# Hybrid decoder trunk on one core: eight-row norm factors and ACT-queue weights at the opening, another place for turning x and a halved last tile at the end

## Chip, cores and metric

One core of a Trainium2 chip runs the whole program in one launch. The metric is device time in microseconds (us), median over runs. One execution was also profiled; its span is the time from the first to the last instruction that the profile shows, and the execution's own time is a little longer than that. In what follows PE is TensorE (matrix products and transposes), PEld its weight loads, DVE VectorE, ACT ScalarE, POOL GpSimd, and SP SyncE, which here only issues DMAs. "SPq" and "POOLq" are DMAs issued by SP and POOL.

## The reference

Two layers over 512 tokens of width 1024. Each layer has a half-step SwiGLU block, a mixing block with three groups of heads, and another half-step SwiGLU block:

```python
for l in range(DEPTH):
    x = x + 0.5 * swiglu(rms_norm(x, ffn1_norm[l]), ffn1_w_in[l], ffn1_w_out[l])
    h = rms_norm(x, mix_norm[l]) @ w_mix_in[l]
    ...
    x = x + y @ w_mix_out[l]
    x = x + 0.5 * swiglu(rms_norm(x, ffn2_norm[l]), ffn2_w_in[l], ffn2_w_out[l])
return x
```

with `rms_norm(x, gain) = x * rsqrt(mean(x*x) + eps) * gain` and `swiglu(h) = (silu(gate) * up) @ w_out`, where gate and up are the two halves of `h @ w_in` (2 x 2816 columns). All is float32. The change concerns the very first block (layer 0, ffn1) and the very last one (layer 1, ffn2), and the loads of the norm gains in between.

## The kernel before

**Products.** Every operand is split into a high and a low part (`hi`, `lo`, in a rounded 32-bit form), and `mm3` makes three PE products of each: hi by hi (L346), hi by lo (L352), lo by hi (L353). `parted` makes the parts of streamed weights: ACT copies the rounded high part (L334), DVE subtracts it for the low part (L335).

**x.** Inside the kernel x lies transposed: `xT` has eight tiles of 128 features by 512 tokens. x comes from memory as tokens by features, so at the opening `load_x` loads the columns of one feature tile (one 256-KB DMA, L1543, into `xs`) and PE turns them with four 128x128 transposes into a PSUM bank (L1546). At the end `turn_x` turns `xT` back (L1509: 8 output tiles with four transposes each) and ACT copies each bank out (L1514).

**Streaming.** `stream` and `stream_steps` walk over the rows of a weight matrix in granules of two row tiles. `granule` loads one into a buffer `st` (two buffers, issued by SP, L315), parts it into `hl` (three buffers), and the products of four jobs (four PSUM banks) follow. Without the flag `end` the order is row tile by row tile, and within each the jobs; in the last granule it is job by job, so that the banks finish one after the other.

**The first block's opening.** `cover` streams the first six tiles of the hidden width in three rounds (f = 0, 2, 4). In the first (`opening`) the callback `pre` is `open_x`: at granule k it applies the gain to x's tiles k and k + 1 out of PSUM (`norm_part`: ACT's high part L420, DVE's low part L421) and, halfway through the granule, loads and turns the next two, copies x to `xT` (L1535) and adds up squares (L431, L434, L435). The gain of a norm is loaded by `begin_norm` (L409) into a tile of 128 partitions by 8, feature k*128 + p at partition p, column k: 1024 single elements from memory. `signs` (L632) makes a negated copy, `ngain`. While `open_x` works, `build_consts` fills masks on DVE and POOL. The `table` call that loads ACT's function table is the program's first statement.

The norm itself is not applied before the products. After the first round `squares` (L454) sums the squares over features into a bank with the tag `po`, ACT and DVE form the reciprocal root (L461 to L446, ending on DVE), and later steps multiply it in. The second round's fourth job writes a bank with the same tag, of which there is one.

**The order.** `follow` chains instructions of one engine into the order of the program text; where it isn't used, a scheduler orders them by priority. From the third round on most work follows a plan (`halved`, `plan`) with the loads `w` (L785, L703) chained on SP's queue. That part isn't touched.

**The last block's end.** In `ffn`, after `cover`, six row tiles of `w_out` remain, streamed in three granules for each half `dg` of the output columns. The last block computes tokens by features directly: first `turn_x` is issued as a whole, its banks all of one tag with two or three banks (`("mm", "sc")[self.ntog % 2]`, here `sc`, two banks), then 72 products for each half into four banks (`mm`, `mm`, `mm`, `po`, then `sc`, `sc`, `pt`, `pt`). DVE adds half of each bank to x (L504) and SP writes the 128x512 tile out (L508).

Of the kernel before, what the change touches and what calls it, by code (L numbers as in the profile page):

```python
# [23 lines left out]
P = 128  # L24
# [157 lines left out]
class Trunk:  # L182
# [32 lines left out]
    def build_consts(self, scratch):  # L215
# [40 lines left out]
        for l in range(1, 7):  # L256
            nc.vector.tensor_scalar(a, xf, scalar1=float(2 ** (l - 1)), scalar2=None, op0=ALU.is_ge)
# [22 lines left out]
    def table(self, name):  # L280
# [5 lines left out]
        self.tab = p.ins.name  # L286
# [15 lines left out]
    def granule(self, parts, kk, ahead=True, skew=0, keep=False):  # L302

# [8 lines left out]
        at = 0  # L312
        for ap in parts:
            w = ap.shape[1]
            nc.sync.dma_start(s3[:, :, at : at + w], ap.rearrange("(k p) c -> p k c", p=P))  # L315
            at += w
        with self.tc.high_priority() if ahead else ExitStack():
            hi, lo = self.parted(st[:, : kk * c], 1 if ahead else kk, skew, keep)
# [3 lines left out]
    def parted(self, src, pieces=1, skew=0, keep=False):  # L322
# [9 lines left out]
        for c in range(0, n, w):  # L332
# [28 lines left out]
    def stream_steps(self, jobs, parts_of, act, nk, mid=None, pre=None, deal=None, keep=False):  # L361
# [11 lines left out]
        while k < nk:  # L373
            kk = min(2, nk - k)
            if callable(mid) and k == nk - 2:
                mid()
            if pre is not None:
# [4 lines left out]
            rows = self.granule(parts_of(k, kk), kk, pre is None, skew, deal is not None)  # L382
            end = k + kk == nk
            order = (
                [(job, j) for job in jobs for j in range(kk)]
                if end
                else [(job, j) for j in range(kk) for job in jobs]
            )
            for n, ((acc, cols, toks, *more), j) in enumerate(order):
# [4 lines left out]
                first, last = k + j == 0 and not more, end and j == kk - 1  # L394
                if toks is None:
                    self.mm3(acc, hi[:, cols], lo[:, cols], ah, al, first, last, False, keep)
                else:
                    self.mm3(acc, ah[:, toks], al[:, toks], hi[:, cols], lo[:, cols], first, last)
# [7 lines left out]
    def begin_norm(self, gain_ap):  # L406
        nc = self.nc
        self.gain = self.const.tile([P, KD], F32, tag="gain", name=self.n("gain"), bufs=2)
        nc.sync.dma_start(self.gain, gain_ap.rearrange("(k p) -> p k", p=P))  # L409
        self.sqacc = None  # L410

# [54 lines left out]
    def ffn(self, w_in, w_out, next_gain, covered, mean=None, begin=None, out=None):  # L466
# [5 lines left out]
        with tc.tile_pool(name=self.n("ffn"), bufs=1) as fp:  # L472
# [11 lines left out]
            if last:  # L484
                xs = self.turn_x()
            for dg in range(2):
# [7 lines left out]
                self.stream(  # L494
# [5 lines left out]
                )  # L500
                if last:
                    for i in range(4):
                        o = self.xo[dg * 4 + i]
                        nc.vector.scalar_tensor_tensor(  # L504
                            out=o, in0=banks[i], scalar=0.5, in1=xs[dg * 4 + i],
                            op0=ALU.mult, op1=ALU.add,
                        )
# [1092 lines left out]
```

## Time and profile before

| | |
|---|---|
| median of 3 runs | 1847.46 us (1845.98 to 1848.6) |
| profiled execution, its own time | 1847.27 us |
| its span | 1845.3 us |
| PE busy in it | 1826.9 us, 99% |
| DVE, ACT, POOL busy | 80%, 55%, 10% |
| bytes moved by DMA | 254 MB, mean 138 GB/s |

The page of the profile lists busy times by engine, the span in 40 slices, DMA queues, the chain of work that ended last, and groups of instructions with mean durations. Other views of the same trace show instructions in order of time, waits with what ended them, and busy times in chosen stretches. PE's products overlap in its pipeline, so that the spacing of their starts, not their listed duration, is what one costs.

### The profile page before, as it was taken

The page shows a single profiled execution, that of the slowest core. Times are in us where ns is not written, and L with a number is a line of the kernel's source. Part 1 is how long each engine was busy: PE and PEld are TensorE (multiplying, and loading weights), DVE is VectorE, ACT ScalarE, POOL GpSimd, SP SyncE. Part 2 cuts the span into 40 slices and gives each one's busy share as a digit, 9 for nine tenths or more (in the row PEclk, how much of TensorE's full clock was granted, in tenths as well). Part 3 has the DMA queues.
Part 4 walks back from the last instruction along what each step waited for, and adds up shares of the span by engine and source line. Part 5 has one row for each costly group of instructions (what it writes and reads, how often), then busy time and mean ns, then how long its engine had stood idle before and what let it go on. Part 6 is the DMA issues. An engine that isn't in the chain of part 4 may idle for free.

```text
span 1845.3 us, 33378 instructions
## 1 busy us (share of the span) xinstructions
PE 1826.9 (99%) x13532; PEld 1698.6 (92%) x13532; DVE 1476.5 (80%) x2101; ACT 1005.9 (55%) x1462; POOL 182.5 (10%) x186
## 2 busy tenths in 40 slices
PE   8999999999999999999999999999999999999999
PEld 6899999899877899999889999998998788999997
DVE  7889787678787988879678887966868878888883
ACT  4455554564665555555445555545546665555552
POOL 0011120100000101112001111201000001020210
PEclk9999999999999999999999999999999999999999
DMA  7658783332323767868276787823323238677762
GB/s 205 183 126 194 178 177 92 69 96 72 76 75 98 215 136 175 186 169 172 81 201 139 169 188 184 172 61 89 81 64 87 81 103 228 151 158 195 150 137 91
DMA packets 247529, 254.00 MB, mean 138 GB/s; under 512 B 19632, under 2 KB 232112, under 8 KB 247376
## 3 DMA queue, kind: packets, MB, share of 16 engines
q1 hardware_dynamic: 191664, 183.69, 33.4%
q0 software_dynamic: 55712, 68.18, 23.2%
q8 instruction: 106, 1.74, 0.4%
q14 instruction: 47, 0.39, 0.1%
HBM read 226.08 MB, written 2.10 MB: 124 GB/s over the span
## 4 chain that ended last, share of the span: by engine, by line
PE 91%; DVE 4%; ACT 3%; issue 1%; DMA 1%; SPq 0%; ACTq 0%; DVEq 0%
PE mm L346 13%; PE mm L353 13%; PE mm L352 13%; PE sc L346 6%; PE sc L353 6%; PE sc L352 6%; PE pt L346 6%; PE pt L352 6%; PE pt L353 6%; PE po L346 3%; PE po L352 3%; PE po L353 3%; PE po L1449 1%; DVE hl L335 1%; ACT hl L334 1%
## 5 line engine op out<-in xcount | busy, mean ns | idle before, releaser
L732 ACT CAST hl<-w 128x1024 fp32r<-128x1024 f32 x322 | 337.7, 1050 | 346.9 <-PE mm L353 81.7
L734 DVE TENSOR_TENSOR hl<-w,hl 128x1024 fp32r<-128x1024 f32 x322 | 392.7, 1220 | 86.5 <-ACT hl L732 86.4
L335 DVE TENSOR_TENSOR hl<-st,hl 128x512 fp32r<-128x512 f32 (+2 forms) x196 | 166.5, 851 | 118.3 <-ACT hl L334 117.3
L334 ACT CAST hl<-st 128x512 fp32r<-128x512 f32 (+2 forms) x196 | 146.6, 750 | 206.9 <-PE mm L353 67.4
L346 PE MATMUL mm<-xc,hl 128*128 128x256 f32 (+1 forms) x730 | 201.3, 276 | 0.3 <-ACT g L831 0.3
L353 PE MATMUL mm<-xc,hl 128*128 128x256 f32 x728 | 201.2, 276 | 0.0
L352 PE MATMUL mm<-xc,hl 128*128 128x256 f32 x728 | 201.1, 276 | 0.0
L346 PE MATMUL sc<-xc,hl 128*128 128x256 f32 (+1 forms) x530 | 146.3, 277 | 0.6 <-ACT g L831 0.6
L353 PE MATMUL sc<-xc,hl 128*128 128x256 f32 x528 | 146.0, 277 | 0.0
L352 PE MATMUL sc<-xc,hl 128*128 128x256 f32 x528 | 145.9, 276 | 0.0
L346 PEld LDWEIGHTS mm<-xc,hl 128*128 128x128 f32 x730 | 137.1, 188 | 0.8 <-ACT g L831 0.5
L353 PEld LDWEIGHTS mm<-xc,hl 128*128 128x128 f32 x728 | 136.7, 188 | 0.1
L352 PEld LDWEIGHTS mm<-xc,hl 128*128 128x128 f32 x728 | 136.7, 188 | 0.0
L352 PE MATMUL pt<-xc,hl 128*128 128x256 f32 x480 | 132.6, 276 | 0.0
L346 PE MATMUL pt<-xc,hl 128*128 128x256 f32 (+1 forms) x482 | 132.6, 276 | 0.0
L353 PE MATMUL pt<-xc,hl 128*128 128x256 f32 x480 | 132.5, 276 | 0.0
L346 PE MATMUL mm<-hl,x 128*128 128x256 f32 (+1 forms) x384 | 112.4, 293 | 0.7 <-DVE ft L442 0.3
L346 PE MATMUL mm<-x,hl 128*128 128x512 f32 x272 | 109.7, 403 | 0.0
L353 PE MATMUL mm<-hl,x 128*128 128x256 f32 (+1 forms) x384 | 107.6, 280 | 0.0
L352 PE MATMUL mm<-hl,x 128*128 128x256 f32 (+1 forms) x384 | 107.3, 279 | 0.0
L353 PE MATMUL mm<-x,hl 128*128 128x512 f32 x272 | 106.5, 392 | 0.0
L352 PE MATMUL mm<-x,hl 128*128 128x512 f32 x272 | 106.0, 390 | 0.0
(470 smaller groups left out, 5677.1 us busy)
## 6 DMA issues: line engine op xcount, KB each, us to landing
w<-in_ffn_w_in_dram SPq DMA_DIRECT2D x140, 512.0 KB, 5.7
w<-in_ffn_w_out_dram SPq DMA_DIRECT2D x64, 512.0 KB, 4.4
w<-in_ffn_w_out_dram POOLq DMA_DIRECT2D x56, 512.0 KB, 8.9
st<-in_w_mix_in_dram SPq DMA_DIRECT2D x88, 256.0 KB, 2.7
w<-in_ffn_w_in_dram POOLq DMA_DIRECT2D x39, 512.0 KB, 8.4
st<-in_ffn_w_in_dram SPq DMA_DIRECT2D x72, 256.0 KB, 3.3
w<-S POOLq DMA_DIRECT2D x35, 512.0 KB, 4.7
st<-in_ffn_w_out_dram SPq DMA_DIRECT2D x24, 512.0 KB, 4.1
```

The costliest lines, as they stand in the source:

```text
L334: a = nc.scalar.copy(hi, src[:, c : c + w])
L335: b = nc.vector.tensor_sub(lo, src[:, c : c + w], hi)
L346: i = nc.tensor.matmul(acc[:, c], ah, bh[:, c], start=first and c.start == 0, stop=False, skip_group_check=True,)
L352: nc.tensor.matmul(acc, ah, bl, start=False, stop=False, skip_group_check=True)
L353: i = nc.tensor.matmul(acc, al, bh, start=False, stop=last, skip_group_check=True)
L732: A(nc.scalar.copy(hi, src))
L734: return lambda: V(nc.vector.tensor_sub(lo, src, hi))
L1449: nc.tensor.matmul(self.ob[:, t0 + u * P : t0 + 2 * P], V[:, j, h % 4].rearrange("p a d -> p (a d)"), part[:, j, u:, :].rearrange("p i t - ...
```

## The change

At the opening:

- The gain of the first norm is loaded as eight rows of 128 (`gr`, 8 DMA rows of 512 bytes in place of 1024 elements), first on SP's queue; PE transposes it and DVE copies it into `gain`.
- The first granule of weights is issued by ACT, in four DMAs of 128 KB (one for each row tile and part), ahead of ACT's table load, which moves from the program's first statement to this place. SP's queue is put into one order by `follow`.
- x's tile k + 1 is scaled between the two halves of the granule's parting (`between`), so that ACT and DVE take tile k, weights k, tile k + 1, weights k + 1.
- DVE's work on one of the masks is put behind the first granule's parting (`first_rows`).
- In the second round the first granule is done job by job (`lead`).

At the end:

- `turn_x` becomes a generator that turns four tiles at a time, over two banks each of `sc` and `pt`, one step after each of the first two granules.
- In the last granule of the second half the last job's products are done in two halves of 256 columns, and its tile is added and written in two halves (`last`).

Between them, the later gains' loads are chained on SP's queue (`follow` in `begin_norm`); they come after the loads `w` of the block that precedes them, where they came earlier before, and the negated copies on DVE move with them.

```diff
-    def granule(self, parts, kk, ahead=True, skew=0, keep=False):
+    def load_rows(self, parts, kk, queue=None):
...
+        for k in [slice(i, i + 1) for i in range(kk)] if queue is nc.scalar else [slice(0, kk)]:
+            at = 0
+            for ap in parts:
+                w = ap.shape[1]
+                d = (queue or nc.sync).dma_start(
+                    s3[:, k, at : at + w], ap.rearrange("(k p) c -> p k c", p=P)[:, k, :]
+                )
+                at += w
+                if queue is not None:
+                    self.follow("a" if queue is nc.scalar else "s", d)
+        return st[:, : kk * c]
...
+            if pieces > 1 and c == 0:
+                self.between()
...
             if pre is not None:
+
+                if k == 0:
+                    st = self.load_rows(parts_of(k, kk), kk, self.nc.scalar)
+                    self.table(LNEXP)
+                    self.follow("a", self.tab_ins)
                 pre(k)
...
-                if end
+                if end or lead and k == 0
...
+            if halves:
+                acc, cols, toks = jobs[-1]
+                for c in (slice(0, T // 2), slice(T // 2, T)):
+                    for j in range(kk):
+                        ah, al = act(k + j)
+                        hi, lo = rows[j]
+                        self.mm3(
+                            acc[:, c], ah[:, toks], al[:, toks], hi[:, c], lo[:, c], False, j == kk - 1
+                        )
...
-        nc.sync.dma_start(self.gain, gain_ap.rearrange("(k p) -> p k", p=P))
         self.sqacc = None
+        if pool is None:
+
+            self.follow("s", nc.sync.dma_start(self.gain, gain_ap.rearrange("(k p) -> p k", p=P)))
+            return
+        g = pool.tile([KD, P], F32, tag="S", name=self.n("gr"), bufs=2)
+        self.follow("s", nc.sync.dma_start(g, gain_ap.rearrange("(k p) -> k p", p=P)))
+        b = self.bank("pt")
+        self.follow("p", nc.tensor.transpose(b[:, :KD], g, self.ident[:KD, :KD]))
+        self.follow("v", nc.vector.tensor_copy(self.gain, b[:, :KD]))
...
-                xs = self.turn_x()
+                xs = []
+                turn = self.turn_x(xs, (("mm", "mm"), ("sc", "pt"))[self.ntog % 2])
...
+                    last=last and dg == 1,
+                ):
+                    if last:
+                        next(turn, None)
...
+                        cs = [slice(0, T)]
+                        if dg and i == 3:
+                            cs = [slice(0, T // 2), slice(T // 2, T)]
...
+                self.begin_norm(gain, fp)
                 self.xb = {j: self.load_x(x, j, fp) for j in (0, 1)}
-                self.begin_norm(gain)
-            for j in (k, k + 1):
-                self.norm_part(j, fp, self.xb[j], 0)
+            self.norm_part(k, fp, self.xb[k], 0)
+
+            self.between = lambda: self.norm_part(k + 1, fp, self.xb[k + 1], 0)
             return
```

More of the change, by code (lines that the diff above doesn't have):

```diff
@@ L359, in stream, with stream_steps @@
             pass
[L361 removed]
+    def stream_steps(self, jobs, parts_of, act, nk, mid=None, pre=None, deal=None, keep=False, lead=False, last=False):
         k = 0
@@ L599, in cover @@
                 None if opening else (lambda k, f=f: deal(2 * f + k // 2)), begin is None or f > 2,
+                lead=f == 2 and begin is not None,
             )
```

63 lines of the change are left out of this document (36 added, 27 removed).

## Prediction

> **What bounds the kernel now.** I read the page first, then stretches of busy time at both ends, the chain of waits there, and the instructions in order of time.
>
> ```profile
> span 1845.3 us, 33378 instructions
> PE 1826.9 (99%) x13532; PEld 1698.6 (92%) x13532; DVE 1476.5 (80%) x2101; ACT 1005.9 (55%) x1462; POOL 182.5 (10%) x186
> ```
>
> TensorE (PE) sets the time. No product is removed, so only places where PE waits or runs slowly can pay: 18.4 us in all (1845.3 - 1826.9), part of it in the middle, where the change puts nothing but small gain loads. The run profiled took 1847.27 us, 1.97 more than its span, and lies 0.19 under the median of the runs, 1847.46. I work from 1847.27.
>
> ```profile
> 8.45:13.60 5.15, 5.15 (x16) 4.22 (x17) 5.14 (x10) 2.19 (x4) 0.00 (x0) 1.00 1.10 316
> 13.60:35.60 22.00, 22.00 (x107) 18.34 (x106) 19.56 (x44) 11.90 (x19) 1.44 (x1) 1.00 0.85 233
> 35.60:41.00 5.40, 4.60 (x18) 3.13 (x18) 3.73 (x6) 4.18 (x5) 0.00 (x0) 1.00 0.47 151
> 1800.00:1803.75 3.75, 3.75 (x35) 3.75 (x35) 3.75 (x4) 1.66 (x2) 0.00 (x0) 1.00 0.35 125
> 1803.75:1810.20 6.45, 5.77 (x41) 4.55 (x40) 1.94 (x3) 4.95 (x8) 0.00 (x0) 1.00 0.53 171
> 1810.20:1841.55 31.35, 31.31 (x138) 25.56 (x137) 8.33 (x11) 3.75 (x4) 0.00 (x0) 1.00 0.19 67
> 1841.55:1845.30 3.75, 0.00 (x0) 0.00 (x0) 0.69 (x1) 0.00 (x0) 0.00 (x0) 1.00 0.37 140
> ```
>
> Columns: stretch, length, busy time and count of PE, PEld, DVE, ACT, POOL, clock, DMA share, GB/s. From 8.45 to 35.60 PE has no gap. The losses are: ahead of 8.45; a slow pace until about 13.6, which this view's clock column does not show; 0.8 us after 35.60; the stretch 1803.75 to 1810.20, whose 5.77 also counts PE's pipelined overlap; and the 3.75 us behind the last product.
>
> **The opening.** In order of time, then from the chain:
>
> ```profile
> 0.75 1.28 ACT L282 ACT_TABLE_LOAD   x1 [0.75 <-PEq L1585]
> 1.80 0.51 SPq L409 DMA_DIRECT2D gain<-in_ffn_norm_dram  x1
> 2.35 1.52 SPq L315 DMA_DIRECT2D st<-in_ffn_w_in_dram  x2
> 3.91 1.75 SPq L1543 DMA_DIRECT2D xs<-in_x_dram  x2
> 6.31 1.26 ACT L420 ACTIVATE x<-mm,gain 128x512 fp32r<-128x512 f32 x2 [4.27 <-DMA gain<-in_ffn_norm_dram]
> 7.74 1.14 ACT L334 CAST hl<-st 128x512 fp32r<-128x512 f32 x2 [0.16 <-DMA st<-in_ffn_w_in_dram]
> 8.45 1.11 PE L1546 MATMUL mm<-ident,xs 128*128 128x128 f32 x4 [2.67 <-DMA xs<-in_x_dram]
> 9.87 0.78 PE L346 MATMUL sc<-x,hl 128*128 128x512 f32 x1
> ...
> 9.56 0.66 PE po L1546 x3
> 10.22 0.43 PE sc L346
> 14.72 0.23 PE sc L346
> 20.20 0.87 PE mm L1546 x8
> ...
> 16.31 1.44 POOL L707 DMA_DIRECT2D w<-in_ffn_w_in_dram  x1 [14.66 <-DMA w<-in_ffn_w_in_dram]
> ```
>
> ACT waits for the gain until 6.31, PE for the third tile of x until 8.45, and the first product starts at 9.87. A product takes 0.43 us at first and 0.23 later (0.2275 as a mean: 31.35 us for 138 in the stretch from 1810.20); a transpose takes 0.22 slow and 0.109 fast (0.66 for three, 0.87 for eight). The twelve products of x's first tile and the eight transposes of x's third and fourth tiles are over at 14.72.
>
> Now the eight rows of factors go out first on SP, and the four loads of the first granule leave SP for ACT. So x's third tile is issued after one small load and two tiles, some 1.7 us earlier (four issues near 0.5 us put it near 2.2, against 3.91). Does it land so much earlier? The bytes bound that:
>
> ```profile
> 1.75:4.00 2.25, 0.31 (x2) 0.34 (x3) 1.11 (x8) 0.28 (x1) 0.00 (x0) 1.00 0.86 232
> 4.00:8.45 4.45, 1.78 (x9) 1.09 (x7) 2.17 (x14) 1.98 (x4) 0.00 (x0) 1.00 0.89 252
> 10.00:15.00 5.00, 5.00 (x17) 3.95 (x16) 3.69 (x6) 1.92 (x4) 0.00 (x0) 1.00 1.12 319
> ```
>
> Before 8.45 the engines moved 2.25 x 232 + 4.45 x 252 = 1643 KB. Three tiles of x and the first granule are 1311 KB (five times 256 KB, in thousands). At the mean of 245 GB/s that takes 5.35 us from 1.75, so 7.1; at 319 it is 5.9. To either comes the time from last packet to semaphore, some 0.5 us by my estimate (the output tile shown below is issued behind DVE's end at 1842.24, lands 2.0 later, and its packets end by 1843.8). That gives 6.4 to 7.6, and 8.0 if later tiles mix in. I take 7.3, nearer the slow end, because the 512-byte packets of x are in the slow rows. Two slow transposes bring the first product to **7.75**.
>
> The operands must be there. The factors: one load's landing is at most 4.4 us in the opening (the wait above ends at 6.2 after an issue at 1.80), so 5.2 at worst, then a transpose and a copy of 8 columns, 0.3 to 0.5 each counting handover; 6.2 at worst. ACT issues four loads at 0.5 to 0.76 each (SP's 1.52 for two) and loads its table (1.28): free by 5.1. Then a cast of x (0.63) and one of weights (0.57): 7.4 at worst, before the first product. No row shows a DMA issued by ACT.
>
> The pace: PE worked without a gap from 8.45, and sped up near 13.6, 5.15 us later. By the same bytes, shared equally between the queues, x's first tile is there near 4.5 (524 KB moved) and its second near 6.2 to 6.5 (1048 KB). If the gapless run now starts with the second at 6.2, the pace rises at 11.3. From 7.75, eight products at 0.43 end at 11.2, four at 0.2275 at 12.1, six transposes at 0.109 at 12.75. Against 14.72 that is **2.0 us**. Lower end: the pace rises at 13.6 as before and the start slips to 8.5: twelve products at 0.43 end at 13.7, six transposes at 14.3, 0.4. Upper end: start at 7.2, and the run counts from x's first tile at 4.5, so fast from 9.65: 3.0.
>
> The Trainium skill ("TensorE: Matmul & The Clock Gate", section "Part 1: The HAM clock gate (the "warmup" mystery)") says that the array runs at half rate until a free-running window of about 3.4 us has been busy, so the moment hangs on the window's phase and not on the first matmul alone. By that rule the rise is 3.4 to 6.8 us after steady work begins, an estimate of 9.6 to 13.0 here, and the opening would bring 1.2 to 3.0 instead of 2.0. The trace's 5.15 agrees with it.
>
> Behind that nothing should stall: the loads of the second x group and granule keep their places ahead of the 512-KB prefetches, and those prefetches move later on SP.
>
> **The first norm's wait.** Chain after the sum of squares (35.60 to 36.47, x2):
>
> ```profile
> 35.60 0.87 PE po L454 x2
> ...
> 39.51 0.70 DVE nt L442
> ...
> 40.25 0.50 PE po L346
> ```
>
> The fourth job's bank (po) holds the sum until DVE's L442 has read it at 40.21, 3.74 us after the sum's end. From 36.47 to 40.75 PE does 14 products, worth 3.19 of 4.28 us: 1.09 lost; by idle time 0.80 (the row 35.60:41.00). Afterwards the granule runs job by job: 18 products, 4.10 us, come ahead of po, more than 3.74. Gain **0.95**, ends 0.8 and 1.09; with the cover of 0.36 us gone it would shrink by what is missing.
>
> **Turning x at the end.**
>
> ```profile
> PEld sc L1509 <- ACT xt L1514: 1.6, 3, 1.1
> L1514 ACT COPY xt<-sc 128x512 f32<-128x512 f32 x8 | 4.6, 585 | 0.7 <-PE sc L1509 0.3
> ...
> 1803.99 0.69 DVE L819 SCALAR_TENSOR_TENSOR xT<-mm,xT 128x512 f32<-128x512 f32 x1 [0.21 <-PE mm L353]
> ```
>
> All eight tiles go through two banks, and PE waits for ACT's copies. Of the stage's 144 products 138 come later; six products (1.37) and 32 transposes (3.49) are 4.86 us of work in 6.45: 1.6 lost. Four tiles now follow the first granule and four the second, over four free banks. ACT has 24 products, 5.46 us, for four copies (2.34) and a cast. The products that now open the stage meet one bank still in use, until 1804.68; by allocation it is the third's turn, 1.37 us after 1803.75. Gain **1.6**, low end 0.7 (the stretch's idle time).
>
> **The last tile in halves.**
>
> ```profile
> 1841.55 0.69 DVE xt L504
> ...
> L643 DVE SCALAR_TENSOR_TENSOR xn<-xT,gain,inv 128x256 f32<-128x256 f32 x32 | 13.4, 479 | 0.1
> ...
> out_dram<-xt SPq DMA_DIRECT2D x8, 256.0 KB, 2.0
> 1842.90:1843.90 1.00, 0.00 (x0) 0.00 (x0) 0.00 (x0) 0.00 (x0) 0.00 (x0) 1.00 0.69 262
> ```
>
> The last six products become twelve of 256 columns, at the same total: the row from 1800.00 has 35 of that width in 3.75 us, 0.107 each, against 0.2275. Behind the last one DVE does half a tile: 0.69 - 0.48 = 0.21. All 262 KB of the last tile move within that last microsecond, at a share of 0.69, in 0.7 to 0.9 us; half saves some 0.4. The first half is summed and issued while PE works on the second. Gain **0.6**; ends 0.2 (packets of 1 KB no faster) and 0.7. The tail of completion stays.
>
> **Moved small loads.** The later gains now stand behind the prefetches on SP, and DVE's ngain moves with them (three places). I cost them at nothing:
>
> ```profile
> 285.57 0.37 SPq L703 DMA_DIRECT2D w<-in_ffn_w_out_dram  x1
> 290.17 1.22 DVE L734 TENSOR_TENSOR hl<-w,hl 128x1024 fp32r<-128x1024 f32 x1
> 292.23 1.22 DVE L734 TENSOR_TENSOR hl<-w,hl 128x1024 fp32r<-128x1024 f32 x1 [0.84 <-ACT hl L732]
> DMA to landing us min/median/max: 2.1/3.3/5.6
> ```
>
> At the first place two gains are issued from 285.94 to 286.9 and land by 292.1 at worst. DVE asks at 291.4 and idles 0.84 there anyway. Queued behind ngain are subtractions for weights; with three hl buffers a finished one waits out at least one product group of 24, 2.6 us at 0.107.
>
> **The sum.** 2.0 + 0.95 + 1.6 + 0.6 = 5.15. 1847.27 - 5.15 = **1842.1 us**. Low ends together gain 2.1 (1845.2), high ends 6.4 (1840.9).
>
> **Rivals.** The fourth draws on this row of the page (loads by queue, median us to landing):
>
> ```profile
> w<-in_ffn_w_out_dram POOLq DMA_DIRECT2D x56, 512.0 KB, 8.9
> ```
>
> 1. The pace rises no earlier than 13.6. Products from 7.75 end at 12.9, four transposes at 0.22 at 13.8, two at 0.109 at 14.0: the opening brings 0.7, the total is 3.85: 1843.4. For it: one transition is seen, and no cause in the trace. Against: PE is busy much earlier.
> 2. x's tiles are bound by bytes, since both queues feed the same engines, already 0.86 to 0.89 busy. The second lands near 8, the third at 8.4 as before; the first product starts at 8.85, eleven products at 0.43 reach 13.6, one more and six transposes 14.5: 0.2, total 3.35, 1843.9. Against: 1643 KB had been moved by 8.45 and 1311 are needed. The Trainium skill ("DMA: Bandwidth & Descriptors", section "Issuing engines are not separate DMA queues") says that loads from several engines share 16 engines and that only issue time is saved, which speaks for this rival.
> 3. ACT's issues are slow, like POOL's 1.44 us in this opening: ACT is free at 7.8, the first product starts at 9.0, 1.25 later than forecast: 1843.4. Against: SP's loads of this kind take half that.
> 4. Slower, through ngain: If a gain lands d us after issue, DVE stands from d = 5, and PE stalls once d exceeds 8.4 (0.84 idle and 2.6 of buffers more). From d = 10.1 three places eat the 5.15; at 13 they cost 13.8: 1855.9. For it: loads on POOL's queue take 8.9 to land. Against: gains on SP never passed 5.6.
> 5. The turning and the halves bring nothing, since PE waits for something else there: 1844.3.
>
> **How the numbers follow.** Forecast 0.68, rivals 0.12, 0.08, 0.04, 0.04, 0.04. About 0.2% (3.7 us, 1843.8) is what a measurement of this kernel tells from no change; its three runs span 1845.98 to 1848.6. The forecast lies 1.7 beyond and holds "faster" nine times in ten; rivals 1 and 3 lie at the edge and count 60 to 40, rival 2 for 40 to 60; rival 5 is no change, rival 4 slower. Faster 0.61 + 0.13 = 0.74, no change 0.21, slower 0.05. Range 1839.8 to 1845.2: the bounds, and at the fast end 1.3 us more for the runs' spread.
>
> **What would show it.** Right: a first product before 8.2, pace 0.23 before 12, the sum of squares done near 34.5; no gap before po; no wait of x's turning for ACT's copies; a last DVE row of 128x256 near 0.45; ngain with no wait over 1 us. Wrong: PE gaps between the first granules, ACT's casts waiting on its own loads past 8, slow products beyond 13, or PE stalls near 292, 932 and 1202.

## The result and the profile after

The changed kernel takes 1844.83 us (median of 12 runs, 1843.96 to 1847.47); the kernel before, on the same chip, 1848.35 (12 runs, 1845.98 to 1849.61). The ratio is 0.9984 with a 95% interval of 0.9976 to 0.9992: some 3.0 us faster (1848.35 x 0.0016; the medians lie 3.52 apart), where 5.15 were forecast. In a second session of 11 runs the ratio was 0.9987 (0.9978 to 0.9996), 2.4 us.

The profiled run of the changed kernel is the slowest of its twelve, 1847.47 us. Its page, span and first lines:

```profile
span 1845.4 us, 33407 instructions
PE 1828.1 (99%) x13539; PEld 1700.3 (92%) x13539; DVE 1476.9 (80%) x2103; ACT 1005.1 (54%) x1462; POOL 182.5 (10%) x186
```

The span is no shorter than before, and PE is busy 1.2 us longer than its 1826.9, though the change adds only seven instructions to it (six by halving products, one small transpose). So this one run has to be read stage by stage, and what it shows of chance has to be told from what it shows of the change.

**Opening.** The chain of waits of the changed kernel (start, us, what):

```profile
2.24 5.71 DMA xs<-in_x_dram
7.95 0.04 issue
7.99 0.69 PE mm L1609 x2
8.68 0.43 PE sc L364
...
11.67 0.37 PE pt L370
12.04 0.23 PE pt L371
...
13.62 0.23 PE sc L364
```

x's third tile is issued at 2.24, as forecast, but lands only at 7.95. The first product starts at 8.33 (the chain counts from the end of the transposes, 8.68), the quick pace of 0.23 begins near 11.8, and the twelve products with their eight transposes are over at 13.62 instead of 14.72. ACT's four issues are cheap (1.84 us for all, in order of time):

```profile
0.75 1.84 ACTq L318 DMA_DIRECT2D st<-in_ffn_w_in_dram  x4
```

Busy time by stretch shows the bytes (last two columns: share of the DMA engines, GB/s; the clock ahead of them reads 1.00 where the trace has no record of it, as up to 11.83 here):

```profile
0.75:3.00 2.25, 0.24 (x1) 0.18 (x1) 1.83 (x13) 0.38 (x1) 0.87 (x4) 1.00 0.52 81
3.00:5.40 2.40, 0.00 (x0) 0.00 (x0) 1.67 (x12) 0.90 (x1) 0.00 (x0) 1.00 1.00 305
5.40:8.00 2.60, 2.24 (x9) 1.44 (x9) 0.70 (x2) 1.36 (x3) 0.00 (x0) 1.00 1.16 305
36.00:41.00 5.00, 3.88 (x17) 2.91 (x16) 4.26 (x9) 4.63 (x6) 0.00 (x0) 1.00 0.36 109
```

Up to 8.0 they moved 2.25 x 81 + 5.00 x 305 = 1707 KB, 0.4 MB more than the 1311 that were waited for.

**The first norm.** The last of those rows still has a hole: PE is busy 3.88 of 5.00 us. The chain there, and PE's longest wait in that stretch (us in total, times, longest):

```profile
31.38 5.45 DMA st<-in_ffn_w_in_dram
...
36.92 1.05 ACT hl L350
37.98 0.59 ACT nr L294
...
38.61 1.22 DVE hl L351
...
40.03 0.61 DVE nt L489
40.64 0.04 issue
40.69 0.50 PE po L364
```

```profile
PE po L364 <- DVE nt L489: 1.1, 1, 1.1
```

The sum of squares starts at 34.42 (35.44 before) and takes 1.02, so it is over 1.0 earlier than in the kernel before, but the fourth bank is free only at 40.64, later than there (40.21). A weight load that lands at 36.8 is split by ACT ahead of the norm's first step, and DVE's half of a split stands ahead of its last. The 18 products that now come first run out at 39.6, and PE waits.

**The later factor loads** are issued where the order now puts them, DVE's negation waits for them, and PE does not (SP in order of time; then, of the negation's row, what its engine was idle for: us in total, times):

```profile
285.29 0.50 SPq L451 DMA_DIRECT2D gain<-in_mix_norm_dram  x1
285.84 0.57 SPq L451 DMA_DIRECT2D gain<-in_ffn_norm_dram  x1
```

```profile
  DMA gain<-in_ffn_norm_dram: 1.7, 2
```

**Two long stretches of PE are slower**, and no wait explains it. First the changed kernel, then the kernel before, by stretch:

```profile
286.00:308.00 22.00, 22.00 (x189) 22.00 (x189) 18.08 (x20) 13.62 (x16) 0.00 (x0) 1.00 0.14 25
870.00:892.00 22.00, 22.00 (x195) 22.00 (x195) 18.44 (x21) 14.46 (x17) 0.00 (x0) 1.00 0.11 26
1198.00:1220.00 22.00, 22.00 (x189) 22.00 (x188) 17.99 (x21) 13.31 (x14) 0.00 (x0) 1.00 0.12 21
```

```profile
286.00:308.00 22.00, 22.00 (x196) 22.00 (x196) 18.56 (x20) 14.45 (x17) 0.00 (x0) 1.00 0.08 25
1198.00:1220.00 22.00, 22.00 (x196) 22.00 (x196) 18.58 (x20) 13.20 (x14) 0.00 (x0) 1.00 0.10 34
```

PE is full in all of them at a clock of 1.00, and still makes 189 products in 22 us in two places and 195 or 196 elsewhere. Product by product the starts are 118 ns apart instead of 113 there; each place costs 0.93. Both begin at the products beside which the two factor loads above are issued, which made those loads the first suspect.

**The end.** The stage of the last output opens with 24 products, PE no longer waits for ACT's copies of x, and the stage ends 1.35 us nearer to its start. Behind the last product (chain of the changed kernel, and DVE's group of rows there):

```profile
1841.39 0.13 PE pt L371
1841.52 0.02 issue
1841.55 0.42 DVE xt L559
```

```profile
L559 DVE SCALAR_TENSOR_TENSOR xt<-pt,xt 128x256 f32<-128x256 f32 (+1 forms) x3 | 1.4, 509 | 1.4 <-PE pt L371 1.4
```

The half whose products come first is summed only from 1841.55, behind the last product of the second half. Both halves' sums then follow one another, 0.76 in all against 0.69 for the whole tile.

### The profile page after: what moved, and what is told of

Same layout as the page of the kernel before. It is cut to its first block, busy times and chain, and to the rows that moved or that the text cites. A ratio compares the mean times of both kernels' runs of the same rounds, so it can differ in the third digit from the quotient of the medians.

```text
span 1845.4 us, 33407 instructions
## 1 busy us (share of the span) xinstructions
PE 1828.1 (99%) x13539; PEld 1700.3 (92%) x13539; DVE 1476.9 (80%) x2103; ACT 1005.1 (54%) x1462; POOL 182.5 (10%) x186
## 4 chain that ended last, share of the span: by engine, by line
PE 92%; DVE 4%; ACT 2%; issue 1%; DMA 1%; SPq 0%; DVEq 0%; ACTq 0%
PE mm L364 14%; PE mm L371 13%; PE mm L370 13%; PE sc L364 6%; PE sc L371 6%; PE sc L370 6%; PE pt L370 6%; PE pt L364 6%; PE pt L371 6%; PE po L364 3%; PE po L370 3%; PE po L371 3%; PE po L1508 1%; PE pt L1549 1%; DVE hl L351 1%
```

## Experiments

All are compared by the start of the same product in two traces. "Opening" below is where PE stands at 33 us against the first profile of the kernel before (negative: ahead), "norm" what is added from 33 to 50, "slow" the number of 118-ns stretches (in four places, near 284, 868, 1196 and 1780), "turn" what is added from 1803 to the stage's last tile, "tail" from the last product's end to the span's end, all in us.

```
kernel           first product  opening  norm   slow  turn   tail   median (runs)   ratio to before, 95%
before               9.87         0       0      0     0     3.75   1847.46 (3)
e5 before again     10.20        +0.54  +0.15    3   -0.22   3.75   1850.85 (1)
changed              8.33        -1.02  +0.32    2   -1.35   3.93   1844.83 (12)    0.9984 (0.9976-0.9992)
e1 changed again     8.20        -0.56  -0.61    1   -1.35   3.96   1846.04 (11)    0.9987 (0.9978-0.9996)
e2 loads free        8.14        -1.46  -0.14    0   -1.35   4.05   1844.76 (10)    0.9979 (0.9970-0.9989)
e3 whole tile        8.22        -1.01  -0.57    1   -1.36   4.09   1845.66 (11)    0.9984 (0.9975-0.9993)
e4 no job order      8.42        -1.93  +2.87    0   -1.35   3.95   1846.21 (11)    0.9989 (0.9980-0.9998)
e6 norm ahead        8.56        -0.35  -1.11    0   -1.36   3.96   1844.25 (11)    0.9980 (0.9971-0.9989)
e7 table ahead       7.82        -2.40  -0.62    1   -1.35   3.94   1844.54 (10)    0.9982 (0.9972-0.9991)
e8 weights by SP     8.88        +0.38  -1.07    2   -1.35   3.59   1846.18 (11)    0.9990 (0.9981-0.9999)
e9 two banks         8.54        -0.80  -0.62    2   -1.36   3.49   1844.88 (11)    0.9983 (0.9974-0.9993)
e10 e6 + e7          8.73        -1.48  -0.47    0   -1.36   3.95   1844.38 (11)    0.9980 (0.9971-0.9988)
e11 two sc banks     8.01        -1.81  -0.88    2   -0.75   3.95   1846.19 (11)    0.9991 (0.9982-1.0000)
e12 e6 + e9          8.35        -0.83  -1.10    1   -1.36   3.49   1845.93 (11)    0.9983 (0.9974-0.9992)
e13 rows held        8.04        -1.84  -0.36    2   -1.33   3.95   1845.55 (11)    0.9983 (0.9974-0.9992)
e14 e13 + e6         8.14        -1.01  -1.02    3   -1.33   3.95   1845.50 (11)    0.9980 (0.9972-0.9989)
e15 e7 again         8.79        -0.40  -0.69    0   -1.35   3.96   1844.82 (1)
e16 e13 again        8.17        -1.07  -0.21    3   -1.33   3.94   1847.66 (1)
e17 x held too       7.88        -2.36  -0.39    3   -1.35   3.96   1845.73 (7)     0.9973 (0.9961-0.9984)
e18 e17 again        7.96        -1.96  -1.09    2   -1.33   3.96   1844.64 (1)
```

Sessions ran on different chips, where the kernel before had medians from 1847.94 to 1849.74, so the ratios compare across sessions and the medians do not. All intervals overlap; the verdicts on single terms come from the columns of the traces.

**e1: the changed kernel again.** No edit.

> The changed kernel once more, unaltered, to see which of its first profile's features come back. Theory: all of them. A first product near 8.3 us and the quick pace from near 12; the weight rows of the second round's second granule landing after 36 and PE waiting ahead of po's product near 40.3; two stretches, near 285 to 310 and 1196 to 1220, in which products of 256 columns start 118 ns apart instead of 113; both halves of the last tile summed behind the last product. Time 2.5 to 3.5 us under the kernel before (ratio 0.9981 to 0.9987). Rival: the first profile was one unlucky execution; then the stretches or the late rows are missing, and its span is some 2 us shorter than 1845.4.

A single slow stretch (284), no wait ahead of po, a span of 1844.0. The late first product, the sum of the halves behind the last product and the turn's gain came back; the stretches and po's wait did not come back whole. The theory "all of them" is half wrong: some of the first profile was one execution's.

**e2: the later factor loads let go.**

```
-            self.follow("s", nc.sync.dma_start(self.gain, ...))
+            nc.sync.dma_start(self.gain, ...)
```

> The changed kernel with the later factor loads let go of their given order on SP's queue, so that two of them are issued as early as in the kernel before; nothing else changes on PE or ACT. Theory: their late place (two loads of 1024 packets of 4 bytes each, beside the products near 285 and 1196) is what holds the products at 118 ns; without them the pace is 113 ns there again and the time falls by 1.5 to 2.1 us below the changed kernel, to some 1842.8. Rival 1: the 118 ns follow from the moment at which PE starts again after a short wait, not from the loads: the stretches stay and the time is that of the changed kernel within 0.5. Rival 2, from the prediction: the loads cost nothing in any place; then there is no difference either, and no stretch in either kernel.

No stretch, and 1.3 us less than e1 by the medians of the same session (1844.76 against 1846.04). Taken alone this looks like the theory. The next run takes it away.

**e5: the kernel before again.** No edit.

> The kernel before once more, unaltered, for a second profile. Theory: the stretches of 118 ns near 285 and 1196 belong to the changed kernel, whose factor loads are issued there; this profile has none, and its PE keeps the course of the first within 0.5 us up to 1803. Rival: they come by chance in any kernel that waits there for a moment; then one of the two places may show 118 ns here too.

The rival. The kernel before, by stretch, in this second profile:

```profile
286.00:308.00 22.00, 22.00 (x195) 21.94 (x195) 18.58 (x21) 14.68 (x16) 0.00 (x0) 1.00 0.08 25
870.00:892.00 22.00, 22.00 (x189) 22.00 (x188) 17.91 (x20) 14.43 (x16) 0.00 (x0) 1.00 0.08 25
1198.00:1220.00 22.00, 22.00 (x189) 22.00 (x188) 17.92 (x20) 13.81 (x15) 0.00 (x0) 1.00 0.08 25
```

Three of the four places ran at 118 ns (two of them shown, the third near 1780), with no factor load near them, and the run took 1850.85. Over all profiles here the kernel before had 0 and 3, the changed kernel and its variants 25 in 18, 1.4 each, and the kernel before alone has shown both 0 and 3. The loads are not needed for a stretch. What starts a stretch was not found; those near 284 and 1196 begin behind a PE wait of some 0.1 us at the same product, and in other executions the same wait has no such sequel.

**e3: the last tile whole.**

```
-                    last=last and dg == 1,
+                    last=False,
...
-                        if dg and i == 3:
+                        if False:
```

> The changed kernel with the last output tile whole again (four products of 512 columns at its end, one sum, one store). Theory: the first half can't be summed while products of the second half still write the same bank, so halving saves next to nothing: last product to end of span 3.7 us against 3.85 with halves, time within 0.3 us of the changed kernel, either way. Rival, the prediction's term: halving saves 0.6, so this kernel is 0.6 us slower.

0.4 us below e1 in the same session, inside the intervals: the runs show no gain of the halves. In the traces the last landing is seen 2.77 us behind the last product's end, 2.68 with halves, 2.79 in the kernel before: 0.1 won. PE pays 0.07 for it, since the twelve products of 256 columns start 0.120 apart (1.44) where six of 512 take 1.365.

**e9: each half its own bank.**

```
+                if last and dg:
+                    spare = self.bank("po")
+                    pieces = [(bk, slice(0, T), c) for bk, c in zip(banks[:3], spans)]
+                    pieces += [(b[:, c], c, spans[3]) for b, c in ((banks[3], slice(0, T // 2)), (spare, slice(T // 2, T)))]
...
-                                out=o[:, c], in0=banks[i][:, c], scalar=0.5,
+                                out=o[:, c], in0=(spare if c.start else banks[i])[:, c], scalar=0.5,
```

> The changed kernel with the two halves of the last tile in two banks, all 18 products of that tile made as 36 of 256 columns. Theory: in the changed kernel the first half's sum waits for the last product because both halves stand in one bank; with a bank each it runs while PE makes the second half, the second half's sum starts right behind the last product and its store is issued some 0.5 us after that product's end instead of 0.9. The last landing then comes 2.3 us behind the last product's end instead of 2.7, and PE pays 0.1 to 0.25 for the narrower products: 0.1 to 0.3 us won in all. Rival 1: the first half's sum still starts only behind the last product (another wait); then nothing is won and PE's price is lost. Rival 2, the prediction's term in full: 0.6 won.

As the theory has it. DVE's groups at the end of this kernel (busy, mean ns, idle before and what ended it):

```profile
L563 DVE SCALAR_TENSOR_TENSOR xt<-pt,xt 128x512 f32<-128x512 f32 (+1 forms) x2 | 1.1, 558 | 0.7 <-PE pt L371 0.7
...
L563 DVE SCALAR_TENSOR_TENSOR xt<-po,xt 128x256 f32<-128x256 f32 x1 | 0.4, 424 | 0.3 <-PE po L371 0.3
```

The first half (in pt) follows the tile before without a wait of its own; only the second (in po) waits for the last product. Its store is issued 0.49 behind that product's end instead of 0.91, the landing is seen after 2.22 instead of 2.68, the tail falls from 3.95 to 3.49. PE pays 0.24 more for the narrow products: 0.2 won, a third of the prediction's 0.6. From the first product of this half of the columns to the end of the span, the traces have 20.50 us in the changed kernel, 20.28 here, 20.58 with the whole tile (e3) and 20.23 in the kernel before.

**e11: turning over two banks instead of four.**

```
-                turn = self.turn_x(xs, (("mm", "mm"), ("sc", "pt"))[self.ntog % 2])
+                turn = self.turn_x(xs, (("mm", "mm"), ("sc", "sc"))[self.ntog % 2])
```

> The changed kernel with the second four tiles of x turned over the two sc banks only, instead of sc and pt: the same place behind the first granules, two banks instead of four. Theory: each pair of tiles after the first waits for ACT's copy of 0.585 us against 0.44 us of transposes, so PE loses 0.5 to 1.0 us of the 1.35 that the stage won. Rival: the place alone brings the gain, ACT keeps up, and the loss is under 0.3.

The stage wins 0.75 instead of 1.35: 0.6 lost, as the theory has it. Of the turn's gain a little more than half comes from its place behind the products, the rest from the banks.

**e4: without the job order.**

```
-                lead=f == 2 and begin is not None,
+                lead=False,
```

> The changed kernel without the job-by-job order in the second round's first granule. Theory: with the order, PE still waits ahead of po, because the norm's steps start late (ACT's split of weight rows that land after 36 stands ahead of them), so the order saves only a part: this kernel is 0.2 to 0.7 us slower. Rival 1, the prediction's term: 0.95 us slower. Rival 2: the order saves nothing at all since the late rows bound the next granule anyway: no difference.

By medians 0.2 above e1, inside the intervals, so the runs don't tell what the order is worth; in its profile far worse. PE waits 2.0 us ahead of po, and then this (by stretch; the third number from the end is the granted clock):

```profile
36.00:41.00 5.00, 2.96 (x13) 2.08 (x12) 4.86 (x11) 3.99 (x5) 0.00 (x0) 0.97 0.49 144
41.00:44.00 3.00, 3.00 (x9) 2.32 (x8) 1.41 (x4) 0.20 (x1) 0.00 (x0) 0.50 0.33 109
```

Behind the wait the clock is halved for 3.4 us (40.67 to 44.08 in the trace's record of the clock), with products at 0.43. This execution had the best opening of the unaltered ones (1.93) and lost it all. Only 14 products stand ahead of po here, and DVE's read came 4.98 us behind the sum's end. A short opening alone does not bring such a wait: e18, 1.96 ahead at 33 us, read 3.56 behind the sum and had none.

**e6: the norm ahead of the splits.**

```
-        7: "norm, x 0 0", 8: ...
+        5: "norm", 7: "x 0 0", 8: ...
```

The numbers are steps of the plan, in the order in which ACT and DVE take them.

> The changed kernel with the norm's steps of the second round (three on ACT, three on DVE) put two granules earlier in their given order, ahead of the splits of the second and third granule. Theory: what holds po's product at 39.6 to 40.7, whether the opening ended early or late, is ACT's and DVE's place for the norm behind splits of weight rows that land at 34 to 37; put ahead of them it starts with the sum (end near 35.8) and DVE's last read of po ends before 39, so no gap ahead of po's product, in any execution, and no new wait over 0.3 us for the second granule's split. PE at 50 us is then ahead of the kernel before by the opening's gain plus 0.95, 1.6 to 2.9. Time 0.3 to 0.8 us below the changed kernel. Rival: the late rows themselves hold PE; then the wait moves to the second granule's products (start after 40.5) and nothing is won.

No gap, and no new one behind it (chain; the row by stretch):

```profile
39.77 0.23 PE mm L370
40.00 0.23 PE mm L371
40.23 0.23 PE po L364
```

```profile
36.00:41.00 5.00, 5.00 (x24) 4.11 (x23) 3.28 (x6) 4.77 (x6) 0.00 (x0) 1.00 0.01 5
```

po's product follows in its turn at 40.23. The norm's column reads -1.11 here, -1.10 in e12, -1.02 in e14 and -0.47 in e10, where 0.63 was lost again ahead of the sum of squares; without the edit it lies between -1.09 and +0.32, mean -0.53 of 13 profiles. What the edit takes away is the spread: from the sum's end to DVE's read of it the four profiles with the edit need 2.78 us each, those 13 need 3.56 to 5.19, and PE waits ahead of po in the ten of them that need more than the 4.1 us which the 18 products cover. The median of 1844.25 against 1847.94 of before is the best of that session, though e7's 1844.54 lies within the intervals.

**e7, e15: ACT's table load ahead of its four loads.**

```
-                    st = self.load_rows(parts_of(k, kk), kk, self.nc.scalar)
-                    self.table(LNEXP)
                     self.follow("a", self.tab_ins)
+                    st = self.load_rows(parts_of(k, kk), kk, self.nc.scalar)
...
-        self.table(LNEXP)
+        if self.tab_users: self.table(LNEXP)
...
-    k = Trunk(ctx, tc)
+    k = Trunk(ctx, tc); k.table(LNEXP)
```

> The changed kernel with ACT's table load moved back to its head, so that ACT issues the four loads of the first weight rows from 2.03 on instead of 0.75; nothing else moves. Theory: in the changed kernel these loads run ahead of x's tiles, which were issued from 1.22 but moved hardly a byte before 3, with 59 to 64 GB/s in that gap; without them x's first tile lands near 4.0 instead of 5.1 to 5.5, the third before 7.5 instead of 7.9 to 8.1, and the first product starts at 7.6 to 7.8. Rival 1: bytes bind, and the third tile lands at 7.9 to 8.1 whatever the order; first product 8.2 to 8.4. Rival 2: x comes earlier but the weight rows later, and ACT's cast of them makes the first product later than 8.4.

> The changed kernel with ACT's table load ahead of its four loads, once more. Theory (bytes): the move alone changes little, the first product starts at 7.8 to 8.7 as the two profiles with it had. Rival (ACT's loads ahead of x): 7.8 again.

A first product at 7.82 in e7 and 8.79 in e15, 8.73 with e6's edit in e10. The first looked like the theory; the repeats take it away. ACT's loads running ahead of x are not what delays it, or not alone.

**e8: the first weight rows by SP, between x's second and third tile.**

```
-                    st = self.load_rows(parts_of(k, kk), kk, self.nc.scalar)
+                    st = None
...
-            if st is not None:
+            if pre is not None and k == 0:
```

> The changed kernel with the first weight rows issued by SP again, as two loads behind x's first two tiles and ahead of its third; factors as eight rows first and all else as changed. Theory: ACT's queue is no help, as the first product waits for x's third tile in PE's order; first tile of x near 3.9, weight rows near 5.8, third tile near 7.3, first product 7.6 to 7.9, and 0.3 to 0.6 us won. Rival 1, bytes bind: third tile at 7.9 to 8.1, first product 8.2 to 8.4, no difference. Rival 2, SP's issues bind: the third tile is issued at 3.4 instead of 2.2 and lands after 8.4, first product after 8.7, 0.4 us or more lost.

Its second rival: PE's rows in order of time,

```profile
8.54 0.69 PE L1609 MATMUL mm<-ident,xs 128*128 128x128 f32 x2 [2.50 <-DMA xs<-in_x_dram]
8.88 0.78 PE L364 MATMUL sc<-x,hl 128*128 128x512 f32 x1
```

x's first tiles land by 4.07, yet the third only at 8.5. In this one profile the first product comes 0.6 us behind the mean of nine profiles with ACT's queue (8.31), and 0.3 behind the latest of them (8.56): the queue does help.

**e10 and e12: edits together.**

> The changed kernel with the two edits that helped in their profiles: the norm's steps ahead of the splits, and ACT's table load ahead of its four loads. Theory: they act in different places and add: first product at 7.6 to 7.9, no gap ahead of po's product, PE at 50 us ahead of the first profile of the kernel before by 2.6 to 3.6, wherever the quick pace begins between 9.4 and 13; time 0.5 to 1.3 us below the changed kernel, 3.5 to 4.5 below the kernel before. Rival: with the opening shorter the second granule's rows land too late for PE, and a wait of 0.5 us or more appears behind the norm.

> The changed kernel with the norm's steps ahead of the splits and the last tile's halves in two banks. Theory: both gains hold together, 0.3 to 1.1 us for the norm and 0.2 for the halves: no gap ahead of po's product, last landing 2.2 to 2.3 us behind the last product, span less the number of 118-ns stretches times 0.95 near 1841.5; time 0.5 to 1.0 us below the changed kernel, 3.7 to 4.5 below the kernel before. Rival: the norm's gain only shifts a wait to the sum of squares; then PE at 50 us is not further ahead than in the first profile of the changed kernel (0.7) and the time is that of the changed kernel.

In both po's gap is gone. In e10 the first product missed (8.73), and PE waits for DVE ahead of the sum of squares, which costs 0.63 there: DVE becomes the next limit. e12 keeps -1.10 and the tail of 3.49; its ratio, 0.9983, cannot be told from the changed kernel's.

**e13, e16, e14: the second weight rows held until ACT has cast x's first tile.**

```
+                if queue is nc.sync and self.late:
+                    self.tc.add_manual_dep(d.ins, self.late, SYNC, reason="held")
```

(`SYNC` stands for the dependency's class, which is shortened here, and `self.late` is ACT's instruction that casts x's first tile; it is set elsewhere.)

> The changed kernel with SP's loads of the second weight rows (512 KB) held until ACT has cast x's first tile, near 6.5, so that only x's four tiles and the first weight rows move before. Theory: bytes of later loads delay x's third tile in the changed kernel (1707 KB moved by 8.0 against 1311 needed); held back, the third tile lands by 7.4 and the first product starts at 7.5 to 7.8, 0.5 earlier; the second rows land near 10 and are not needed before 13. PE at 33 us is 0.3 to 0.7 further ahead than the changed kernel's mean of some 1.1. Rival: ACT's loads running ahead of x set it; then third tile at 7.7 to 8.2 and first product at 8.0 to 8.6 as in the changed kernel.

> The kernel with the second weight rows held, once more, for a second profile: first product at 7.5 to 7.8 if later bytes are the cause, 8.0 to 8.6 if not.

> The same with the norm's steps ahead of the splits. Theory: both act, first product at 7.5 to 7.8, no gap ahead of po's product, time 0.7 to 1.4 us below the changed kernel. Rival: first product at 8.0 to 8.6, and only the norm's part is won.

First product at 8.04, 8.17 and 8.14, against a mean of 8.31 in nine profiles of the unaltered opening (8.01 to 8.56). The direction is the theory's, the size of 0.2 a third of it; the rival's range holds all three, and they lie within the spread of the nine, so this edit alone shows no gain.

**e17, e18: x's fourth tile held as well.**

```
+        if j == 3: self.tc.add_manual_dep(d.ins, self.hold, SYNC, reason="held")
```

> The changed kernel with x's fourth tile and the second weight rows held until ACT has cast x's first tile. Theory: the queue moves the third and fourth tile side by side, so 1573 KB had to move where the prediction counted 1311; at 305 GB/s behind 3.0 that is 0.85 us. With the fourth held the third tile lands at 6.9 to 7.3 and the first product starts at 7.3 to 7.7. Rival: ACT's loads ahead of x, or the slow start before 3.0, set it alone; then the first product stays at 8.0 to 8.2.

> The same kernel once more, for a second profile: first product at 7.3 to 7.7 by the theory, 8.0 to 8.2 by the rival.

7.88 and 7.96, outside both ranges, 0.4 below the mean of 8.31. The chain of e18:

```profile
1.70 4.76 DMA xs<-in_x_dram
6.46 0.05 issue
6.51 1.80 PE mm L1613 x6
8.31 0.43 PE sc L366
```

Here the third tile is no longer waited for (in e17 for 0.03 us). Now the second is, which lands at 6.46, and six slow transposes stand ahead of the product. e17's ratio, 0.9973, is the lowest of all, though its interval still meets the changed kernel's.

## Why the prediction was right and wrong

Right were the sign, the stages in which the time lies, and the turning. Wrong were the size and the time: 1842.1 was forecast, 1844.83 measured. Of these 2.7 us, 1.6 are missing gain (5.15 less 3.52 between the medians) and 1.1 the point it was taken from (1848.35 less 1847.27). The steps that failed are the landing of x's third tile (7.3 forecast, 7.95 in the first profile), the norm's 3.74 us that 18 products were to cover (5.2 there), and the first half's sum beside the products of the second (it came behind them).

**The point it was taken from.** The prediction subtracts from one execution, "1847.27", and notes how it stands to three runs. That execution had no 118-ns stretch; the second one profiled had three, and over all twenty profiles the mean is 1.4, at 0.93 each. The medians of the kernel before, 1847.94 to 1849.74 in six later sessions, all lie above the execution profiled. That part of the miss was chance read as a base.

**Opening: 2.0 forecast, 1.1 measured** (mean of nine profiles, 0.35 to 1.93, against the profile that the sum was made from; 1.4 against the mean of its two). What failed is "I take 7.3, nearer the slow end": the third tile's landing. The sum counted three tiles of x and the first granule, 1311 KB, at 245 GB/s from 1.75. In the trace little moved before 3.0 (81 GB/s), then 305 GB/s, shared with x's fourth tile and the next rows; 7.95 is the 8.0 that the text had set aside "if later tiles mix in". Holding those loads back brought 0.2 (within the spread) and 0.4 of the 0.56 us by which the first product was late. That ACT's issues are slow (rival 3) was wrong, 0.46 us each; that bytes bind (rival 2) was right in kind, at half its price.

The late first product accounts for a part of the missing 0.9 only, since ahead of the pace's rise PE works at half pace and half of a delay is lost: 0.28 of 0.56. A second part is the rise itself. The traces' records of the granted clock put it at 9.95 to 13.24 in the nine profiles, 11.8 as a mean against the forecast 11.3, which is worth 0.25 (rises 3.3 us apart made openings 1.6 apart). The second tile of x, from which the prediction counted, was again half a microsecond later than its 6.2 (its first transpose starts at 6.7 as a mean). "5.15 us later" was right as a mean (5.1) and luck in any one execution: the rise comes 3.2 to 6.5 us behind that transpose. A third part is in the sum: 12.75 adds up the starts of products and transposes, while 14.72 is the end of the last transpose in the kernel before; the next product there starts at 14.48, so 0.24 of the 2.0 was never there to win. What is left of the 0.9, some 0.15, was not followed up.

**The first norm: 0.95 forecast, 0.5 measured.** The cost of the wait and the 18 products ahead were counted rightly: with the norm put ahead, 1.1 came out. The step that failed is "18 products, 4.10 us, come ahead of po, more than 3.74". It took the 3.74 us from the sum's end to DVE's read as work that moves with the sum. Part of it is the norm's place behind a split whose rows land when SP's queue brings them; the sum came 1.0 earlier, the read 0.4 later, and 3.74 became 5.2 (35.44 to 40.64); over 13 profiles it was 3.6 to 5.2, and 2.8 with the norm ahead of the splits. With it, "Behind that nothing should stall" fell.

**Turning x: 1.6 forecast, 1.35 measured** in every profile with four banks, against the profile that the sum was made from; the second profile of the kernel before was itself 0.22 quicker in this stage, so against the mean of the two it is 1.24. Place and banks both act, as e11 shows, and no copy of ACT is waited for. The size was 0.25 too large (0.36 against that mean), 0.17 of it because the switches from transposes back to products still cost: at both, two products start 0.31 apart instead of 0.23.

**The last tile in halves: 0.6 forecast, at most 0.1 measured, and the end as a whole 0.3 longer than before.** The step "The first half is summed and issued while PE works on the second" failed. Both halves stand in one bank, and the first sum's row waits for the last product. With two banks (e9) it does run beside PE, and 0.2 is won over the one bank, 0.3 over the whole tile of e3. The bytes' part was too large too: the second store of 128 KB lands 1.8 us behind its issue, the whole tile of 256 KB 2.0. "The tail of completion stays" was wrong by 0.3. SP waits at the end for all its load and store counters in a fixed order, 0.06 us each. Waits of SP in the trace, with the counter's number:

```
before   1844.298 [107]  1844.359 [108]                                    then the drain at 1844.424
changed  1843.722 [100]  1844.192 [102]  1844.254 [103] ... 1844.555 [108]  then the drain at 1844.622
```

In the kernel before the last store's counter is the last but one to be waited for, in the changed kernel six come behind it: 0.43 from landing to drain instead of 0.13. e3 shows this without halves: its whole tile is stored on counter 100, seven waits come behind it, and its tail is 4.09 where the kernel before has 3.75. With one load more on SP (e8) the last store falls on 108 and the tail is 3.59.

**The moved small loads: nothing, as forecast.** The negation waits 0.5 and 1.2 us, 1.7 in all, the second a little over the "no wait over 1 us" of the forecast, and PE waits for none of it. Rival 4 had its mechanism, not its price. Rival 5 was right of the halves and wrong of the turning.

**The sum as measured:** 1.1 + 0.5 + 1.35 - 0.07 (narrow products) - 0.2 (tail, 3.95 against 3.75) = 2.7, beside 2.4 and 3.0 from the ratios; against the mean of the two profiles of the kernel before the terms are 1.4, 0.6 and 1.24, and the sum is 2.9. That leaves nothing that needs another cause.

## What to carry to other kernels

A wait that follows a producer is only worth what the producer's lead is worth if every step between moves with it: look for a step in that chain that is queued behind something timed by another queue, and move that too. Splitting the last tile pays only where the first part has a bank of its own. Take two or three profiles before subtracting from one: here executions of one kernel differ by up to three stretches of 0.93 us, as much as the whole change.

## What the runs showed of the hardware

Products of 256 columns ran at 113 or 118 ns apart for whole stretches of 22 to 25 us at a granted clock of 1.00; the same program did the one or the other by execution, in four places, at 28 of 80 chances in all twenty profiles. No cause was found.

A PE wait of 2.0 us (e4) was followed by 3.4 us at a clock of 0.50; the changed kernel's wait of 1.1 at the same place had no such sequel. The Trainium skill ("TensorE: Matmul & The Clock Gate", section "Part 1: The HAM clock gate (the "warmup" mystery)") has the rate set by how busy a free-running window of about 3.4 us was; the traces agree. In all twenty, the recorded stretches at full clock last a whole number of times 3.413 us (9 and 528 times in e4, 536 or 537 in the others), e4's half-clock stretch in between lasts 3.41, and the same opening reached full clock anywhere from 9.95 to 13.24. The table in that section of the Trainium skill has the array back at half rate after at least one idle window; here a wait of 2.0 us, shorter than a window, was enough.

With four loads on ACT's queue and five on SP's (the factors and four tiles of x) issued between 0.75 and 3.3, the sixteen engines moved 81 GB/s up to 3.0 and 305 from there; of x's 512-byte packets, issued from 1.22 on, only some 15 had moved by 3.0.
